# Decode value matmuls in groups of eight and twelve calls, in one fixed order, with nine page buffers

## The chip, the cores and the metric

The kernel runs on one core of a Trainium2 chip. The metric is the device time of that core in microseconds (us); smaller is better. Engines are named as in the profile: PE is TensorE (PEld its weight loads), ACT is ScalarE, DVE is VectorE, POOL is GpSimd, SP is SyncE. POOL and SP also issue DMA transfers, each through its own queue, in the order of their instructions.

## The reference

One step of a hybrid decoder layer, all in float32: a prompt of 512 rows (with 16 learned rows ahead of it) and eight decode sequences of four new rows each. Both go through one input projection, stick-breaking attention with 8 heads of 128, a gated short convolution, and output projections. A decode sequence also reads four pages of 128 old keys and values through a page table.

```python
h = rmsnorm(x, g_pre)
q, k, v, ga, cb, cc, ch, gc, ma, mc = split(h @ w_in)
a = stick_breaking(q, k_past+k, v_past+v) * silu(ga)     # A[t,s] = sigmoid(z_ts) * prod_{s<j<t}(1 - sigmoid(z_tj))
c = cb * causal_conv3(cc * ch) * silu(gc)
merged = sigmoid(ma + b) * (a @ w_pa) + sigmoid(mc + b) * (c @ w_pc)
y = x + rmsnorm(merged @ w_out, g_post)
```

The part that the change touches is the last product of the decode attention, `attn @ v` over the pages: for each of 8 sequences, 2 halves of the 1024 value columns and 4 pages, a product of the weights (128 keys x 32 rows of head and time) with the page (128 keys x 512 columns), plus the product with the sequence's own four new rows.

## The kernel before, in words

Nearly all matmuls are float32 products made of three single-pass products each (high and low parts of both operands). They stand at L256 (`gemm_into`: key, value and query projections, and later `w_pc` and `w_pa`) and at L941 (`product`, used by `seven`, which makes a 2x2 block product with seven instead of eight products). The program runs: start and norm; projections and the first four heads; the gate and convolution stage (L941), with the decode logits on DVE between; then the **w_pc stage**, a loop over `j` of 16 column blocks, each 48 matmuls at L256 into the PSUM tiles `mm` (three buffers), emptied by DVE at L1148. Into this loop the four last prompt heads are put (`head_here`, at `j` = 0, 3, 6, 9: L608 logits, L677 sums, L687 values), and the **decode value matmuls**, L841, through the generator `decode_steps` (`dec_step`). Then come the w_pa stage (L256 on `a_hl`) and the output projection.

A decode value call is of full precision (plain float32): the stationary operand is `A_all` (128 x 32, named `z_all` in the profile), the moving one a page tile `vpage` (128 x 512). The profile shows each call as two matmul records and two weight loads. A call writes 32 of the 128 PSUM partitions of the tile `tp` and takes one of four column groups of the array, `tile_position=(0, 32 * j)`. Over one `po` (a pair of sequence group `g` and column half `hf`) 16 calls with pages and 4 with `v_new` (the new rows) add up; then ACT copies `po` to `ob` (L846), PE transposes it (L849) and DVE multiplies it into `sg_s` (L854). There are four such `po`, so 80 calls. Pages are loaded by POOL (L730, 256 KB each, 64 loads) into `vpage`, which has seven buffers: a load waits until the call that read its buffer has ended.

The order on each engine is made when the program is built, by a scheduler with a model of time: an instruction goes as soon as the model has its inputs ready, the earlier in the code first. `pin` (`keep_in_program_order`) ties an instruction behind what its engine was given just before it in the code. On the chip each engine takes its instructions strictly in that order and waits where an input is late. Before the change the calls are not pinned, so that each is placed where the model has its page landed.

Of the kernel before, what the change touches and what calls it, by code (L numbers as in the profile page):

```python
# [9 lines left out]
F32 = mybir.dt.float32  # L10
# [7 lines left out]
P = 128  # L18
# [26 lines left out]
NPG = 4  # L45
# [15 lines left out]
def hybrid_step_kernel(  # L61
# [7 lines left out]
    pe, act, dve, pool = nc.tensor, nc.scalar, nc.vector, nc.gpsimd  # L69
# [662 lines left out]
    def decode_steps():  # L732
# [89 lines left out]
        for g in range(2):  # L822
            for hf in range(2):
                cs = slice(hf * 512, (hf + 1) * 512)
                po = t_ps()
                for pg in range(NPG + 1):
                    if pg < NPG:
                        vts = []
                        for j in range(4):
                            vt = d3.tile([P, 512], F32, name="vpage", bufs=7)  # L830
                            page_load(vt, vc, 4 * g + j, pg, cs)
                            vts.append(vt)
                        if g + hf + pg == 0:
                            yield "values"
                    for j in range(4):
                        bb = 4 * g + j
                        if pg < NPG:
                            lhs, rhs = A_all[:, pg, bb].rearrange("p h t -> p (h t)"), vts[j]
                        else:
                            lhs, rhs = An[:, bb, :], vflat[:, cs]  # L840
                        pe.matmul(po[32 * j:32 * (j + 1), :], lhsT=lhs, rhs=rhs, start=(pg == 0),  # L841
                                  stop=(pg == NPG), tile_position=(0, 32 * j), skip_group_check=True)
                    if pg < NPG:
                        yield
                ob = d3.tile([P, 512], F32, name="ob")
                act.copy(ob, po)  # L846
                pt = t_ps()
                for hh in range(4):
                    pe.transpose(out=pt[:, hh * P:(hh + 1) * P], in_=ob[:, hh * P:(hh + 1) * P], identity=ident)  # L849
                for hh in range(4):  # L850
                    h = 4 * hf + hh
                    src = pt[:, hh * P:(hh + 1) * P].rearrange("p (j h t) -> p j h t", h=H, t=DT)[:, :, h, :]
                    ss = slice(16 * g, 16 * (g + 1))
                    dve.tensor_mul(sg_s[:, h, ss].rearrange("p (j t) -> p j t", t=DT), src,  # L854
                                   sg_s[:, h, ss].rearrange("p (j t) -> p j t", t=DT))
                yield
# [4 lines left out]
    def dec_step(n=1, until="end"):  # L861

        for _ in range(n):
            if dec_at & {"end", until}:
                return
            dec_at.add(next(dec, "end"))
# [126 lines left out]
        s = sp2.tile([P, 8, P], F32, name="s")  # L993
        yield from seven(ws, n, rb, rt, s, lambda name: sp2.tile([P, HU], F32, name=name)[:, :n])

    gctx = ExitStack()
    gp = gctx.enter_context(tc.tile_pool(name="gates", bufs=2))
    sp2 = gctx.enter_context(tc.tile_pool(name="sums", bufs=1))


    UP, US = PQ + 2, DB * (DT + 2)
# [4 lines left out]
    def conv_pair(i):  # L1006

        def cv(name):
            return [gp.tile([P, 2, HU], F32, tag=name, name=name, bufs=3) for _ in range(2)]

        cc = cv("cv")
        for m, half, b in pair(COL_CC + i * P, HU):
            act.copy(cc[m][:, half, :], b)
        dec_group()
        us_ = [gp.tile([P, UP + US], F32, name="u", bufs=2) for _ in range(2)]
        for m, half, b in pair(COL_CH + i * P, HU):
            u = us_[m]
            up = u[:, 0:UP]
            us = u[:, UP:].rearrange("p (b t) -> p b t", t=DT + 2)
            if half == 0:  # L1020
                dve.tensor_mul(up[:, 2:HU], b[:, 2:HU], cc[m][:, 0, 2:HU])
            else:
                n = PQ - HQ
                dve.tensor_mul(up[:, 0:2], b[:, 0:2], cc[m][:, 1, 0:2])
                dve.tensor_mul(up[:, HU:UP], b[:, 2:2 + n], cc[m][:, 1, 2:2 + n])
                dve.tensor_mul(us[:, :, 2:], b[:, 2 + n:].rearrange("p (b t) -> p b t", t=DT),
                               cc[m][:, 1, 2 + n:].rearrange("p (b t) -> p b t", t=DT))
        dec_group()
        ys = []
        for m in range(2):  # L1030
            u, ii = us_[m], i + m
            up = u[:, 0:UP]
            us = u[:, UP:].rearrange("p (b t) -> p b t", t=DT + 2)
            act.copy(us[:, :, 0:2], stc[:, ii, :].rearrange("p (b r) -> p b r", r=2))
            y = gp.tile([P, 2, HU], F32, tag="cv", name="cv", bufs=3).rearrange("p a b -> p (a b)")[:, 0:TQ]
            for yv, uv, sl in ((y[:, 0:PQ], up, lambda q: (slice(None), slice(q, q + PQ))),
                               (y[:, PQ:TQ].rearrange("p (b t) -> p b t", t=DT), us,
                                lambda q: (slice(None), slice(None), slice(q, q + DT)))):
                dve.tensor_scalar(out=yv, in0=uv[sl(0)], scalar1=wcv[:, 0, ii:ii + 1],
                                  scalar2=wcv[:, 3, ii:ii + 1], op0=ALU.mult, op1=ALU.add)  # L1040
                for q in (1, 2):
                    dve.scalar_tensor_tensor(out=yv, in0=uv[sl(q)], scalar=wcv[:, q, ii:ii + 1], in1=yv,
                                             op0=ALU.mult, op1=ALU.add)
            lt = gp.tile([P, 18], F32, name="lt", bufs=1)
            act.copy(lt[:, 0:2], up[:, PQ:PQ + 2])
            act.copy(lt[:, 2:18].rearrange("p (b r) -> p b r", r=2), us[:, :, DT:DT + 2])
            pt = t_ps()
            pe.transpose(out=pt[0:18, 0:P], in_=lt, identity=ident)
            ln = gp.tile([18, P], F32, name="ln", bufs=1)
            act.copy(ln, pt[0:18, 0:P])  # L1050
            pool.dma_start(conv_prompt[0, 0, :, ii * P:(ii + 1) * P], ln[0:2, :])
            pool.dma_start(conv_sample.rearrange("o b r c -> (o b r) c")[:, ii * P:(ii + 1) * P], ln[2:18, :])
            ys.append(y)
        for m, half, b in pair(COL_GC + i * P, HQ):
            s = by_query(m, half)
            act.activation(b, b, AF.Silu)
            dve.tensor_mul(ys[m][:, s], b, ys[m][:, s])
        dec_group()
        for m, half, b in pair(COL_CB + i * P, HQ):
            s = by_query(m, half)  # L1060
            dve.tensor_mul(ys[m][:, s], b, ys[m][:, s])
        for m in range(2):
            pool.dma_start(c_scr[i + m], ys[m])
        dec_group()
# [12 lines left out]
        dec_group()  # L1077
    for i in range(0, 8, 2):
        conv_pair(i)


    for j in range(0, KD, 2):
# [51 lines left out]
    for j in range(KD):  # L1134
        if j in HERE:
            head_here(HERE[j])
        dec_step(1 + j % 2)
        if j in HERE:
            k = j // 3
            x = sg_load(k)  # L1140
# [291 lines left out]
```

## Time and profile before

| | before |
|---|---|
| median of 3 runs | 1614.03 us (1613.54 to 1615.36) |
| profiled execution, its span | 1615.1 us, 1.1 us above the median |
| PE busy in it | 1595.0 us (99%) |
| granted TensorE clock, mean | 0.997 |
| decode value matmuls, records | 128 with pages, 32 with `v_new`, from 1149.4 to 1301.8 us |
| page loads | 64 of 256 KB, median 5.4 us from issue to landing |

The profiled execution is the source of all durations below; the span is its own time from the first to the last instruction. A busy PE in these views includes the time in which a matmul waits inside the array for the one before it, so two places with a full PE can differ in what they get done.

### The profile page before, as it was taken

The page shows a single profiled execution, that of the slowest core. Times are in us where ns is not written, and L with a number is a line of the kernel's source. Part 1 is how long each engine was busy: PE and PEld are TensorE (multiplying, and loading weights), DVE is VectorE, ACT ScalarE, POOL GpSimd, SP SyncE. Part 2 cuts the span into 40 slices and gives each one's busy share as a digit, 9 for nine tenths or more (in the row PEclk, how much of TensorE's full clock was granted, in tenths as well). Part 3 has the DMA queues.
Part 4 walks back from the last instruction along what each step waited for, and adds up shares of the span by engine and source line. Part 5 has one row for each costly group of instructions (what it writes and reads, how often), then busy time and mean ns, then how long its engine had stood idle before and what let it go on. Part 6 is the DMA issues. An engine that isn't in the chain of part 4 may idle for free.

```text
span 1615.1 us, 32344 instructions
## 1 busy us (share of the span) xinstructions
PE 1595.0 (99%) x12172; PEld 1533.7 (95%) x12172; DVE 1268.6 (79%) x3574; ACT 754.0 (47%) x1339; POOL 238.0 (15%) x428
## 2 busy tenths in 40 slices
PE   9999999999999999999999999999999999999997
PEld 8999999999999999999999999999757789999997
DVE  6328999947899999999999986667565747887776
ACT  6335554435444444444454444446554523355562
POOL 1133333221111001001011100001322210000000
PEclk9999999999999999999999999999999999999999
DMA  8245555344554445454455544444966755533345
GB/s 244 85 139 179 162 173 177 114 121 142 163 166 138 137 139 164 119 151 133 139 171 183 155 145 128 130 127 124 334 218 222 232 152 162 173 88 110 99 133 187
DMA packets 300675, 252.77 MB, mean 157 GB/s; under 512 B 11522, under 2 KB 268614, under 8 KB 299702
## 3 DMA queue, kind: packets, MB, share of 16 engines
q1 hardware_dynamic: 272021, 160.45, 34.5%
q0 software_dynamic: 28368, 89.98, 16.8%
q8 instruction: 95, 1.56, 0.4%
q14 instruction: 63, 0.51, 0.1%
q10 hardware_dynamic: 128, 0.27, 0.1%
HBM read 217.95 MB, written 32.71 MB: 155 GB/s over the span
## 4 chain that ended last, share of the span: by engine, by line
PE 95%; DMA 2%; DVE 2%; ACT 1%; issue 0%; DVEq 0%; POOL 0%; SPq 0%; ACTq 0%
PE mm L941 31%; PE mm L256 27%; PE o L941 23%; PE tp L841 3%; PE mm L321 2%; PE z L677 1%; PE o L687 1%; PE z L321 1%; PE z L608 1%; PE z L1373 1%; DMA sg<-a_scr 1%; PE tp L505 0%; DMA raw<-in_w_pc 0%; DMA qb<-q_scr 0%; PE z L1227 0%
## 5 line engine op out<-in xcount | busy, mean ns | idle before, releaser
L240 ACT CAST whi<-raw 128x1024 fp32r<-128x1024 f32 x247 | 259.5, 1051 | 385.2 <-PE mm L941 118.5
L241 DVE TENSOR_TENSOR wlo<-raw,whi 128x1024 fp32r<-128x1024 f32 x247 | 301.8, 1223 | 87.8 <-ACT whi L240 86.5
L941 PE MATMUL mm<-h_hi,whi 128*128 128x272 f32 (+1 forms) x1152 | 332.3, 288 | 0.0
L941 PE MATMUL mm<-h_lo,whi 128*128 128x272 f32 (+1 forms) x1152 | 332.3, 288 | 0.0
L941 PE MATMUL mm<-h_hi,wlo 128*128 128x272 f32 (+1 forms) x1152 | 332.3, 290 | 0.0
L941 PE MATMUL o<-t_hi,whi 128*128 128x272 f32 (+1 forms) x864 | 250.1, 289 | 1.6 <-DVE c L967 1.6
L941 PE MATMUL o<-t_lo,whi 128*128 128x272 f32 (+1 forms) x864 | 250.2, 290 | 0.0
L754 DVE CUSTOM_DVE_ANT_0 junk<-kpage,qb 128x128 f32<-128x128 f32 x1024 | 246.3, 288 | 4.7 <-DMA qb<-q_scr 4.3
L941 PE MATMUL o<-t_hi,wlo 128*128 128x272 f32 (+1 forms) x864 | 249.8, 289 | 0.0
L941 PEld LDWEIGHTS mm<-h_hi,whi 128*128 128x128 f32 x1152 | 217.4, 189 | 0.0
L941 PEld LDWEIGHTS mm<-h_hi,wlo 128*128 128x128 f32 x1152 | 216.8, 189 | 0.1
L941 PEld LDWEIGHTS mm<-h_lo,whi 128*128 128x128 f32 x1152 | 216.8, 188 | 0.1
L241 DVE TENSOR_TENSOR wlo<-s,whi 128x1024 fp32r<-128x1024 f32 x126 | 154.4, 1225 | 63.6 <-ACT whi L240 62.4
L240 ACT CAST whi<-s 128x1024 fp32r<-128x1024 f32 x126 | 132.0, 1048 | 153.8 <-PE mm L941 51.7
L256 PE MATMUL mm<-h_lo,whi 128*128 128x280 f32 (+1 forms) x640 | 187.6, 293 | 0.0
L256 PE MATMUL mm<-h_hi,wlo 128*128 128x280 f32 (+1 forms) x640 | 187.1, 293 | 0.0
L256 PE MATMUL mm<-h_hi,whi 128*128 128x280 f32 (+1 forms) x640 | 186.7, 292 | 0.0
L941 PEld LDWEIGHTS o<-t_hi,whi 128*128 128x128 f32 x864 | 163.0, 189 | 2.1 <-DVE c L967 2.0
L941 PEld LDWEIGHTS o<-t_lo,whi 128*128 128x128 f32 x864 | 163.4, 189 | 0.4 <-issue 0.4
L941 PEld LDWEIGHTS o<-t_hi,wlo 128*128 128x128 f32 x864 | 163.1, 189 | 0.1
L256 PEld LDWEIGHTS mm<-h_lo,whi 128*128 128x128 f32 x640 | 120.3, 188 | 0.8
L256 PEld LDWEIGHTS mm<-h_hi,whi 128*128 128x128 f32 x640 | 120.5, 188 | 0.5
(390 smaller groups left out, 3214.5 us busy)
## 6 DMA issues: line engine op xcount, KB each, us to landing
raw<-in_w_in SPq DMA_DIRECT2D x192, 512.0 KB, 4.3
kpage<-in_cache_k POOLq DMA_DIRECT2D x64, 256.0 KB, 3.7
qb<-q_scr POOLq DMA_DIRECT2D x32, 512.0 KB, 5.7
vpage<-in_cache_v POOLq DMA_DIRECT2D x64, 256.0 KB, 5.4
raw<-in_w_out SPq DMA_DIRECT2D x32, 512.0 KB, 4.1
gate_scr<-g POOLq DMA_DIRECT2D x32, 272.0 KB, 4.8
gt<-gate_scr POOLq DMA_DIRECT2D x16, 544.0 KB, 4.5
raw<-in_w_pc SPq DMA_DIRECT2D x16, 512.0 KB, 7.3
```

Source lines behind the costliest of these rows:

```text
L240: act.copy(hi, x)
L241: dve.tensor_sub(lo, x, hi.bitcast(F32))
L256: pe.matmul(o, lhsT=w, rhs=r[:, t0:t1], start=(k == 0 and n == 0), stop=(k == nk - 1 and n == 2))
L321: pin(pe.matmul(o, lhsT=l, rhs=r[:, k, t0:t1], start=(start and m == 0), stop=(stop and m == 2), skip_group_check=True))
L608: pe.matmul(zt[:m, c0:c0 + n], lhsT=l[:, s0:s0 + m], rhs=r[:, ts:ts + n], start=(c0 == 0 and i == 0), stop=(i == 2), skip_group_check=True)
L677: pe.matmul(o, lhsT=l, rhs=x, start=False, stop=(i == len(ops) - 1), skip_group_check=True)
L687: pe.matmul(ot[:, ts - NMETA:ts - NMETA + n], lhsT=l[:m, st, :], rhs=x[:m, c0:c0 + n], start=False, stop=(g == GROUPS[-1] and i == 2), ski ...
L754: dve.tensor_tensor_reduce(out=junk, in0=kt[:, h * P:(h + 1) * P], in1=qt[:, t, h * P:(h + 1) * P], scale=1.0, scalar=0.0, op0=ALU.mult, o ...
L841: pe.matmul(po[32 * j:32 * (j + 1), :], lhsT=lhs, rhs=rhs, start=(pg == 0), stop=(pg == NPG), tile_position=(0, 32 * j), skip_group_check= ...
L941: pe.matmul(o, lhsT=l[:, k, :], rhs=r, start=(start and k == 0 and m == 0), stop=(stop and k == 7 and m == 2), skip_group_check=True)
L1373: pin(pe.matmul(o, lhsT=(m1, m2)[h][:, k + 8 * (q == 1), ts], rhs=two[h][q == 2][:, :, k, :], start=(n == 0), stop=(n == 47)))
```

## The change

The calls over two pages are now handed over together: eight in the first half of a `po`, and twelve in the second (eight with pages and the four with `v_new`). All are pinned, so the scheduler can put nothing between them. In a group the calls stand in the reverse of the order of loading, so that the page loaded last comes first; the column group runs 3, 2, 1, 0, 3, 2, 1, 0. `vpage` has nine buffers instead of seven. The generator now yields 8 times after "values" instead of 20, and the loop over `j` takes one step per `j` instead of one or two. To make room for the buffers, the pools of the gate and convolution stage are put in another order, and the tiles `u`, `lt` and `ln` go to a pool of their own (`convu`), which is closed after the convolution.

```diff
-                for pg in range(NPG + 1):
-                    if pg < NPG:
-                        vts = []
+                def pages(vts, last):
+                    for n, (lhs, rhs, pg, j) in enumerate(vts):
+                        pin(pe.matmul(po[32 * j:32 * (j + 1), :], lhsT=lhs, rhs=rhs, start=(pg == 0),
+                                      stop=last and n >= len(vts) - 4, tile_position=(0, 32 * j), skip_group_check=True))
+
+                for pp in range(0, NPG, 2):
+                    vts = []
+                    for pg in (pp, pp + 1):
                         for j in range(4):
-                            vt = d3.tile([P, 512], F32, name="vpage", bufs=7)
+                            vt = d3.tile([P, 512], F32, name="vpage", bufs=9)
                             page_load(vt, vc, 4 * g + j, pg, cs)
-                            vts.append(vt)
...
-                        pe.matmul(po[32 * j:32 * (j + 1), :], lhsT=lhs, rhs=rhs, start=(pg == 0),
-                                  stop=(pg == NPG), tile_position=(0, 32 * j), skip_group_check=True)
-                    if pg < NPG:
+                            vts.insert(0, (A_all[:, pg, 4 * g + j].rearrange("p h t -> p (h t)"), vt, pp, j))
+                    if g + hf + pp == 0:
+                        yield "values"
+                    if pp == 0:
+                        vts[4:] = [(l, r, 1, j) for l, r, _, j in vts[4:]]
+                    else:
+                        vts += [(An[:, 4 * g + j, :], vflat[:, cs], NPG, j) for j in reversed(range(4))]
+                    pages(vts, pp > 0)
+                    if pp == 0:
                         yield
...
-    gctx = ExitStack()
+    gctx, uctx = ExitStack(), ExitStack()
+    sp2 = gctx.enter_context(tc.tile_pool(name="sums", bufs=1))
     gp = gctx.enter_context(tc.tile_pool(name="gates", bufs=2))
-    sp2 = gctx.enter_context(tc.tile_pool(name="sums", bufs=1))
+    up_ = uctx.enter_context(tc.tile_pool(name="convu", bufs=2))
...
-        dec_step(1 + j % 2)
+        dec_step(1)
```

The built order on PE before the change, in the second of the four `po`, at the end of the first prompt head of the loop (`mm` is the w_pc product, `z` and `o` a prompt head, `tp` the decode value product):

```order
L687 MATMUL o<-loA,vhi 128x512
L687 MATMUL o<-hiA,vlo 128x512
L841 MATMUL tp<-vpage,z_all 32x512
L256 MATMUL mm<-c_hl,whi 128x272
L256 MATMUL mm<-c_hl,wlo 128x272
L256 MATMUL mm<-c_hl,whi 128x272 x2
L841 MATMUL tp<-vpage,z_all 32x512
L256 MATMUL mm<-c_hl,wlo 128x272
L256 MATMUL mm<-c_hl,whi 128x272 x2
```

And on PE after the change, at the end of the first `po` (its second group), where the sums of the second head stand ahead of it:

```order
L677 MATMUL z<-lo,neg_u 128x400
L256 MATMUL mm<-c_hl,whi 128x272 x2
L256 MATMUL mm<-c_hl,wlo 128x272
L256 MATMUL mm<-c_hl,whi 128x272 x2
L256 MATMUL mm<-c_hl,wlo 128x272
L256 MATMUL mm<-c_hl,whi 128x272
L829 MATMUL tp<-vpage,z_all 32x512 x8
L829 MATMUL tp<-v_new,z_new 32x512 x4
L256 MATMUL mm<-c_hl,whi 128x272
L256 MATMUL mm<-c_hl,wlo 128x272
```

Before, single calls stand between w_pc matmuls; now all 80 calls stand in eight such unbroken pieces. The first piece, which stood ahead of the first head's work after 72 w_pc matmuls, now comes after that head's last L687. In the matmuls of other lines that stand between one piece and the next, the new order has 99, 77, 69, 82, 89, 74 and 82.

On POOL before the change (`gate_scr<-gt` stores a finished w_pc product and waits for DVE), each load follows the one call that frees its buffer:

```order
L730 DMA vpage<-in_cache_v 128x512
L1149 DMA gate_scr<-gt 128x544
L730 ISA
L730 DMA vpage<-in_cache_v 128x512
L730 ISA
```

On POOL after the change, ahead of the third group's loads (shown with numbers, since the page tiles of one group have neighbouring ones: 15625 is the last of the second group, 15712 the first of the third):

```order
L730 DMA vpage_15625<-in_cache_v 128x512
L730 ISA
L730 DMA vpage_15712<-in_cache_v 128x512
L1154 DMA gate_scr_890<-gt_16454 128x544
L1154 DMA gate_scr_890<-gt_16554 128x544
L730 ISA
L730 DMA vpage_15714<-in_cache_v 128x512
```

Eight of the nine buffers belong to a group, so only the first page of the next group can be asked for before the group's calls have run; its other seven are asked for behind the calls. Of such stores the new order has 0, 2, 1, 1, 2, 0 and 2 between a group's calls and the last load of the next group.

On PE at the end of the stage, after the change, the last head's values and the first w_pa matmuls (`a_hl`):

```order
L687 MATMUL o<-hiA,vlo 128x512
L256 MATMUL mm<-c_hl,wlo 128x272
L256 MATMUL mm<-c_hl,whi 128x272 x2
...
L852 MATMUL tp<-ident,ob 128x128 x4
L256 MATMUL mm<-c_hl,whi 128x272 x2
L256 MATMUL mm<-c_hl,wlo 128x272
L256 MATMUL mm<-a_hl,whi 128x272 x2
```

Ten w_pc matmuls and the four transposes stand between the two now; before it was 97 w_pc matmuls.

More of the change, by code (lines that the diff above doesn't have):

```diff
@@ L825, in decode_steps @@
                 po = t_ps()
-                for pg in range(NPG + 1):
-                    if pg < NPG:
-                        vts = []
+                def pages(vts, last):
[5 more added lines that the diff above has]
+                    for pg in (pp, pp + 1):
                         for j in range(4):
-                            vt = d3.tile([P, 512], F32, name="vpage", bufs=7)
+                            vt = d3.tile([P, 512], F32, name="vpage", bufs=9)
                             page_load(vt, vc, 4 * g + j, pg, cs)
-                            vts.append(vt)
[L833 to L836, printed above, removed]
-                        if pg < NPG:
[L838 to L841, printed above, removed]
-                                  stop=(pg == NPG), tile_position=(0, 32 * j), skip_group_check=True)
-                    if pg < NPG:
+                            vts.insert(0, (A_all[:, pg, 4 * g + j].rearrange("p h t -> p (h t)"), vt, pp, j))
[7 more added lines that the diff above has]
+                    if pp == 0:
                         yield
@@ L1014, in conv_pair @@
         dec_group()
-        us_ = [gp.tile([P, UP + US], F32, name="u", bufs=2) for _ in range(2)]
+        us_ = [up_.tile([P, UP + US], F32, name="u", bufs=2) for _ in range(2)]
         for m, half, b in pair(COL_CH + i * P, HU):
@@ L1043, in conv_pair @@
                                              op0=ALU.mult, op1=ALU.add)
-            lt = gp.tile([P, 18], F32, name="lt", bufs=1)
+            lt = up_.tile([P, 18], F32, name="lt", bufs=1)
             act.copy(lt[:, 0:2], up[:, PQ:PQ + 2])
@@ L1048, in conv_pair @@
             pe.transpose(out=pt[0:18, 0:P], in_=lt, identity=ident)
-            ln = gp.tile([18, P], F32, name="ln", bufs=1)
+            ln = up_.tile([18, P], F32, name="ln", bufs=1)
             act.copy(ln, pt[0:18, 0:P])
@@ L1079, in hybrid_step_kernel @@
         conv_pair(i)
+    uctx.close()
     for j in range(0, KD, 2):
```

## Prediction

> **What bounds the kernel now.** I read the page's parts 1 and 4 first, then the records of line L841 (the decode value calls) in two stretches, then the timeline of PE at those calls. The page has the span, the busy time of each engine, and the chain of work that ended last by engine and by line:
>
> ```profile
> span 1615.1 us, 32344 instructions
> PE 1595.0 (99%) x12172; PEld 1533.7 (95%) x12172; DVE 1268.6 (79%) x3574; ACT 754.0 (47%) x1339; POOL 238.0 (15%) x428
> PE 95%; DMA 2%; DVE 2%; ACT 1%; issue 0%; DVEq 0%; POOL 0%; SPq 0%; ACTq 0%
> PE mm L941 31%; PE mm L256 27%; PE o L941 23%; PE tp L841 3%; PE mm L321 2%; PE z L677 1%; PE o L687 1%; PE z L321 1%; PE z L608 1%; PE z L1373 1%; DMA sg<-a_scr 1%; PE tp L505 0%; DMA raw<-in_w_pc 0%; DMA qb<-q_scr 0%; PE z L1227 0%
> ```
>
> PE is the bound, and the value calls are themselves on the chain (3% of the span). So time taken off PE there comes off the end, as long as nothing else is late. L841's busy time alone, by stretch (busy time, records, loads, clock, DMA share, GB/s):
>
> ```profile
> 1149.00:1158.00 9.00, 1.91 (x12) 0.39 (x12) 0.81 1.05 356
> 1158.00:1303.00 145.00, 45.55 (x148) 6.40 (x148) 1.00 0.71 222
> ```
>
> Six calls (12 records) cost 1.91 us in the first stretch; the other 74 take 45.55 us. That they differ so much per call (0.32 and 0.62 us) is the matter of this change. The timeline of PE shows why: a lone call, then four calls in a row, then four with pages and four with the new rows (start, duration from the first start to the last end, count of records):
>
> ```profile
> 1163.52 0.28 PE L256 MATMUL mm<-c_hl,wlo 128*128 128x272 f32 x1
> 1163.73 1.05 PE L841 MATMUL tp<-vpage,z_all 128*32 128x512 f32 x2
> 1164.71 0.52 PE L256 MATMUL mm<-c_hl,whi 128*128 128x272 f32 x2
> 1165.06 0.29 PE L256 MATMUL mm<-c_hl,wlo 128*128 128x272 f32 x1
> ...
> 1247.52 0.29 PE L256 MATMUL mm<-c_hl,wlo 128*128 128x272 f32 x1
> 1247.73 1.06 PE L841 MATMUL tp<-vpage,z_all 128*32 128x512 f32 x8
> 1248.73 0.52 PE L256 MATMUL mm<-c_hl,whi 128*128 128x272 f32 x2
> 1249.09 0.28 PE L256 MATMUL mm<-c_hl,wlo 128*128 128x272 f32 x1
> ...
> 1255.31 1.06 PE L841 MATMUL tp<-vpage,z_all 128*32 128x512 f32 x8
> 1256.30 1.06 PE L841 MATMUL tp<-v_new,z_new 32*32 32x512 f32 x8
> 1257.30 0.52 PE L256 MATMUL mm<-c_hl,whi 128*128 128x272 f32 x2
> ```
>
> One call holds the array from 1163.73 to 1164.71; four calls in the four column groups hold it from 1247.73 to 1248.73. Four cost what one costs, and a second round of four adds 0.99 us (1255.31 to 1256.30).
>
> **The change part by part.** First the unit: in steady work 320 matmuls take 40.00 us, 0.125 us each.
>
> ```profile
> 1360.00:1400.00 40.00, 40.00 (x320) 40.00 (x320) 29.85 (x64) 15.58 (x26) 3.71 (x7) 1.00 0.62 189
> ```
>
> Around the lone call, L256 at 1163.52 to L256 at 1165.06 is 1.54 us with three w_pc steps in it (0.375), so a lone call costs 1.165 us: its 1.05 busy and 0.115 of switching in and out. The same at the four calls: 1.57 - 0.375 = 1.195. A group of eight is then 1.195 + 0.99 = 2.185, one of twelve 3.175.
>
> *Removed and put in its place.* After 1158 the 74 calls stand in 39 separate pieces: 45.55 + 39 x 0.115 = 50.0 us. Afterwards 80 calls stand in eight pieces: 4 x 2.185 + 4 x 3.175 = 21.4 us. The difference is **-28.6 us**. The first six calls of before give nothing, since they ran inside a stall that stays:
>
> ```profile
> 1149.36 1.91 PE L841 MATMUL tp<-vpage,z_all 128*32 128x512 f32 x12
> 1154.53 0.82 PE L256 MATMUL mm<-c_hl,whi 128*128 128x272 f32 x2 [3.25 <-DVE gt L1148]
> 1155.14 0.43 PE L256 MATMUL mm<-c_hl,wlo 128*128 128x272 f32 x1
> 1157.41 0.51 PE L256 MATMUL mm<-c_hl,whi 128*128 128x272 f32 x2
> 1142.59 10.63 DMA sg<-a_scr
> ```
>
> The last row is of the chain in order of time: PE waits for DVE to empty `mm`, and DVE waits for a 256 KB load that took 10.63 us. After the change PE has 72 w_pc matmuls, then nothing, until the same moment.
>
> *The first wait.* Nine page loads instead of seven now go out while that load is on its way, in a stretch in which the DMA engines are full:
>
> ```profile
> 1130.00:1140.00 10.00, 10.00 (x76) 9.79 (x75) 6.03 (x9) 6.45 (x10) 2.70 (x5) 1.00 1.09 338
> 1140.00:1150.00 10.00, 10.00 (x84) 9.48 (x84) 5.85 (x9) 9.97 (x18) 4.55 (x7) 1.00 1.08 351
> ```
>
> Two pages are 0.52 MB, at 351 GB/s up to 1.5 us more; but the loads that came at 1150.7 before, behind the first calls, are then gone. Bounds -1 to +1.5; I take **+0.5**, since the full share is the nearest row. After such an idle time the clock is low: from 1154.53 to 1157.41 there are 13 matmuls, 2.88 us instead of 1.63. That 1.25 us is paid before and after alike.
>
> *Waits for pages.* This is the new wait: the whole piece waits for eight pages, and everything behind it on PE with it (w_pc, the heads, then w_pa). POOL's timeline has the nearest case, seven loads freed at once, and the landing times of all pages:
>
> ```profile
> 1234.80 3.78 POOL L730 DMA_DIRECT2D vpage<-in_cache_v  x6 [10.35 <-PE tp L841]
> 1238.97 0.54 POOL L730 DMA_DIRECT2D vpage<-in_cache_v  x1 [0.39 <-issue]
> 1239.52 0.55 POOL L1149 DMA_DIRECT2D gate_scr<-gt  x1
> DMA to landing us min/median/max: 2.8/5.4/7.6
> ```
>
> The seventh load goes out 4.2 us behind the first and lands 5.4 to 7.6 us later. With 1.0 us until the group's first four calls have freed their buffers, the next group is complete 10.6 to 12.8 us from its predecessor's start, plus 0.55 per store that stands ahead in POOL's queue (none, 2, 1, 1, 2, none, 2). What PE has to do until it gets there: 99, 77, 69, 82, 89, 74 and 82 matmuls at 0.125, plus the piece itself: 14.6, 12.8, 10.8, 13.4, 13.3, 12.4 and 12.4 us. So the waits are 0, 0 to 1.1, 0.4 to 2.6, 0, 0 to 0.6, 0 to 0.4 and 0 to 1.5: 0.4 to 6.2 in all. I take **+2.5**, nearer to the median landing. Nine buffers, the reverse order and the smaller step count cost nothing else: the first piece comes behind 310 w_pc matmuls, 39 us of work, and its pages were asked for ahead of these, and a wait at the first call of a piece covers those of the other seven.
>
> [...]
>
> *Chains of the heads.* Lone calls were cover for ACT and DVE too: between the second head's last L608 and the first L677 that needs the chain's result, PE took 20 us, and ACT gave that result at 1207.83; now 83 w_pc matmuls, 10.4 us, stand there.
>
> ```profile
> 1197.71 0.17 PE L608 MATMUL z<-qhi,klo 128*16 128x16 f32 x1
> 1217.70 0.34 PE L677 MATMUL z<-hi,neg_u 128*128 128x400 f32 x1
> 1207.83 0.53 ACT L494 CAST hi<-r 128x416 fp32r<-128x416 f32 x1
> 1313.82 0.69 DVE L1119 TENSOR_TENSOR sg<-o,sg 128x512 f32<-128x512 f32 x1 [3.75 <-PE o L687]
> 1315.90 0.69 DVE L495 TENSOR_TENSOR a_hl<-sg,a_hl 128x512 fp32r<-128x512 f32 x1
> ```
>
> 1208.36 - 1197.88 is 10.5 us: just in time, without the 9 us that were spare. At the stage's end the last head's output needs 2.8 us (1313.82 to 1316.59); ten w_pc matmuls, four transposes and 21 of w_pa cover it with about 4.4. Bounds 0 to 2 us for each of four heads; I take **+2** in all.
>
> *Pools.* The early part of the stage at L941 is put in a slightly other order (`u`, `sums`). PE is full there, so 0, within 1 us.
>
> The sum on the profiled execution: 1615.1 - 28.6 + 0.5 + 2.5 + 2 = 1591.5. It lies 1.1 above the median of the runs, so the forecast is **1590 us**, 1.5% less.
>
> **The rivals.** *Pages bind (B).* If the page loads get only half of the DMA engines throughout, seven of them (1.83 MB at half of 338 GB/s) need 10.9 us, from 1.0 us behind the start and with the 2.8 of the shortest landing: 14.7. The waits are then 0.1, 1.9, 3.9, 1.3, 1.4, 2.3 and 2.3, 13 us instead of 2.5 (the stores go out meanwhile): **1601 us**. For it: the stage's bytes stay, while its time shrinks. Against it: the share after 1158 is only 0.71. [...]
>
> *Cold array (C), the slower side.* If each of the seven waits passes 3.25 us, the idle time at which the trace shows the clock fall, each costs 3.3 + 1.25 us, 32 in all, and with the terms of the first wait and of the heads that is more than the gain: 1614.0 - 28.6 + 32 + 2.5, **1620 us**. It decides from 3.7 us per group, (28.6 - 2.5) / 7, clock included; the share just named speaks against it.
>
> *No packing (D).* Each call in a group waits for its own page; if that kept the calls apart, 80 calls of 0.98 us would cost 79 us, against 50 now: **1644 us**. The four calls at 1247.73 had four pages too, and overlapped.
>
> *Cover gone (E).* The heads and the emptying of `mm` eat the gain: 7 us at each of four heads, **1614 us**. DVE is busy for 93 of the 152 us of this stretch, and could stand 124:
>
> ```profile
> 1149.40:1301.80 152.40, 149.15 (x888) 102.25 (x887) 93.02 (x209) 71.78 (x125) 37.81 (x70) 0.99 0.73 230
> ```
>
> *Better (F).* The load of the first wait comes 1 us earlier, and no piece or chain waits: **1584 us**.
>
> **How the numbers follow.** Forecast 0.62 (own range 1585 to 1596), B 0.20, C 0.05, D 0.03, E 0.05, F 0.05. The range, 1584 to 1604, holds the forecast, F's edge and most of B. About 0.2% (3 us) is what a measurement of this kernel tells from no change. Faster by more: forecast, B and F, 0.87; within: E, with a little of B's tail, 0.05; slower: C and D, 0.08.
>
> **What would show it.** L829 should be eight pieces with about 20.5 us busy, each piece's first record alone with an idle time in front. POOL's waits for PE at `vpage` should fall from 27 to about seven. A piece that runs over 2.2 (eight) or 3.2 us (twelve), idle PE of over 1 us ahead of most pieces, a clock under 1.0 after 1160, or L677 and L687 waiting for ACT or DVE would make the terms wrong in that order.

## The result, and the profile after

The changed kernel takes 1597.6 us (median of 4 runs, 1596.9 to 1598.9), the kernel before on the same chip 1614.7 (1613.5 to 1618.5). The ratio is 0.9897, 95% interval 0.9882 to 0.9913: 17 us faster, where 24 were forecast. Of all the executions behind this document three took 2572, 3063 and 4180 us, and the ratios leave them out. The profiled execution has a span of 1597.3 us against 1615.1.

The page after has the span and the busy time; then comes line L829 (the value calls, L841 of before) in the two stretches used for before (busy time and records of PE, the same of weight loads, granted clock, DMA share, GB/s):

```profile
span 1597.3 us, 32319 instructions
PE 1567.6 (98%) x12172; PEld 1533.7 (96%) x12172; DVE 1268.8 (79%) x3574; ACT 752.7 (47%) x1339; POOL 234.6 (15%) x428
```

```profile
1149.00:1158.00 9.00, 0.00 (x0) 0.00 (x0) 0.76 0.87 290
1158.00:1303.00 145.00, 18.86 (x160) 4.03 (x160) 0.97 0.77 244
```

The same 160 records stand there, in 18.9 us instead of 47.5 (19.4 with the end of the last group, which this stretch cuts off), and no call is left in the first wait. PE's timeline shows one group of eight and one of twelve:

```profile
1200.39 0.40 PE L687 MATMUL o<-hiA,vlo 128*128 128x512 f32 x1
1200.71 1.92 PE L829 MATMUL tp<-vpage,z_all 128*32 128x512 f32 x16
1202.57 0.18 PE L608 MATMUL z<-qhi,klo 128*16 128x16 f32 x1
...
1219.07 0.29 PE L256 MATMUL mm<-c_hl,whi 128*128 128x272 f32 x1
1219.29 1.92 PE L829 MATMUL tp<-vpage,z_all 128*32 128x512 f32 x16
1221.14 1.06 PE L829 MATMUL tp<-v_new,z_new 32*32 32x512 f32 x8
1222.13 0.39 PE L256 MATMUL mm<-c_hl,whi 128*128 128x272 f32 x1
1222.37 0.29 PE L256 MATMUL mm<-c_hl,wlo 128*128 128x272 f32 x1
```

From the w_pc matmul at 1219.07 to the one at 1222.37 is 3.30 us with two w_pc steps in it (0.25), so a group of twelve holds PE for 3.05; eight calls take 0.99 less, 2.06. Four of each are 20.4 us, where 21.4 were forecast and 50.0 stood before. PE's busy time in the whole span fell by 27.4 us (1595.0 to 1567.6), the span by 17.8. What is missing is idle time, and matmuls that ran slowly, which count as busy. The stage of the change shows both, in PE's timeline (in square brackets the idle time ahead, and what ended it) and in windows (stretch, length, busy time of PE, PEld, DVE, ACT and POOL, granted clock, DMA share, GB/s):

```profile
1154.34 0.82 PE L256 MATMUL mm<-c_hl,whi 128*128 128x272 f32 x2 [5.79 <-DVE gt L1153]
...
1179.96 0.52 PE L256 MATMUL mm<-c_hl,whi 128*128 128x272 f32 x2 [2.05 <-DVE gt L1153]
...
1211.42 0.63 PE L256 MATMUL mm<-c_hl,whi 128*128 128x272 f32 x2 [2.29 <-DVE gt L1153]
```

```profile
1140.00:1150.00 10.00, 8.56 (x69) 8.34 (x67) 4.97 (x8) 9.52 (x16) 4.91 (x8) 1.00 1.05 368
1150.00:1160.00 10.00, 5.66 (x25) 5.66 (x26) 5.61 (x10) 0.66 (x2) 0.56 (x1) 0.68 0.86 271
1180.00:1185.00 5.00, 5.00 (x28) 5.00 (x29) 3.55 (x11) 1.49 (x3) 0.54 (x1) 0.66 0.62 191
1206.00:1211.00 5.00, 3.13 (x25) 2.91 (x24) 0.97 (x3) 3.44 (x6) 1.47 (x3) 1.00 0.99 314
1211.00:1216.00 5.00, 4.58 (x24) 4.58 (x25) 3.95 (x9) 2.32 (x4) 0.54 (x1) 0.66 0.96 353
```

All three waits are for the same thing: DVE's multiply of `gt`, which empties `mm`. Behind each of them the granted clock is low (0.68, 0.66 and 0.66 in the windows that begin at 1150, 1180 and 1211). The chain of waits says what kept DVE at the first, DVE's timeline what kept it at the third, and the waits summed over 1139 to 1308 (us in total, times, longest) say how little PE waited for pages:

```profile
1141.71 11.32 DMA sg<-a_scr
1153.15 0.70 DVE sg L1124
1153.85 0.45 DVE gt L1153
1154.34 5.81 PE mm L256 x24
```

```profile
1210.92 0.79 DVE L1153 TENSOR_TENSOR gt<-mm,gt 128x272 f32<-128x272 f32 x2 [4.03 <-DMA gt<-gate_scr]
```

```profile
POOL vpage L730 <- PE tp L829: 39.6, 8, 9.3
PE mm L256 <- DVE gt L1153: 10.1, 3, 5.8
PE tp L829 <- DMA vpage<-in_cache_v: 1.4, 2, 0.7
```

At 1154 the multiply of `gt` stood on DVE behind one that waited 11.3 us for `a_scr`. At 1180 it stood behind a head's chain (DVE was busy without a gap from 1174 on), and at 1211 it waited for a gate tile that SP had asked for only at 1204.01, in the midst of eight page loads (POOL issued them from 1202.06 to 1206.93).

### The profile page after: what moved, and what is told of

It reads as the page before. It is cut to its first block, busy times and chain, and to the rows that moved or that the text cites. A ratio compares the mean times of both kernels' runs of the same rounds, so it can differ in the third digit from the quotient of the medians.

```text
span 1597.3 us, 32319 instructions
## 1 busy us (share of the span) xinstructions
PE 1567.6 (98%) x12172; PEld 1533.7 (96%) x12172; DVE 1268.8 (79%) x3574; ACT 752.7 (47%) x1339; POOL 234.6 (15%) x428
## 4 chain that ended last, share of the span: by engine, by line
PE 89%; DMA 4%; issue 2%; DVE 2%; ACT 1%; POOL 0%; DVEq 0%; POOLq 0%; SPq 0%; ACTq 0%
PE mm L944 32%; PE mm L256 24%; PE o L944 23%; DMA vpage<-in_cache_v 2%; PE mm L321 2%; PE z L321 1%; PE z L677 1%; PE o L687 1%; DMA raw<-in_w_in 1%; PE z L608 1%; PE z L1378 1%; DMA sg<-a_scr 1%; DMA gt<-gate_scr 1%; DVE wlo L241 1%; PE tp L829 0%
```

## The experiments

For each run the ratio is to the kernel before, on the same chip. Beside it I give the length of the stage in the profiled execution, from the start of the first w_pc matmul to that of the last w_pa matmul: 282.1 us before, 265.2 after. It leaves out what differs from execution to execution earlier on (the first w_pc matmul came between 1135.8 and 1140.6 in these traces). Every edit makes the planner, as the scheduler of the build is called below, place the groups anew: the first group stands behind 310 w_pc matmuls after the change, behind 328 with buffers of their own, and behind 269 with the first pages held back. So two runs differ in more than the edit alone.

**The pools and buffers alone.** The kernel before, with `bufs=9` for `vpage` and the three pools changed:

```
-                            vt = d3.tile([P, 512], F32, name="vpage", bufs=7)
+                            vt = d3.tile([P, 512], F32, name="vpage", bufs=9)
-        us_ = [gp.tile(...)]; lt = gp.tile(...); ln = gp.tile(...)
+        us_ = [up_.tile(...)]; lt = up_.tile(...); ln = up_.tile(...)
```

> The kernel before with the changed kernel's nine page buffers and its new pools, but the value calls page by page and not pinned, as before. Theory (the time follows the number of pieces): this order has the 80 calls in 34 pieces, where the order of before has 40; with 0.98 us for a round of up to four calls and 0.2 for switching that is some 7 us less, so about 1607 us. Rival 1 (buffers and pools carry the gain, through pages that come earlier): 1600 or less. Rival 2 (buffers and pools do nothing): 1614.7 within 2.

Measured: 0.9988 (0.9975 to 1.0001), 1613.2 us, stage 281.9. The calls became 6.3 us shorter, as the planner set more of them together, yet the stage stayed as long. The groups of L841 in the stage (busy time, mean ns of one), and a row of PE's timeline:

```profile
L841 PE MATMUL tp<-vpage,z_all 128*32 128x512 f32 x128 | 37.2, 611 | 0.0
L841 PE MATMUL tp<-v_new,z_new 32*32 32x512 f32 x32 | 4.2, 600 | 0.0
```

```profile
1257.42 0.49 PE L677 MATMUL z<-lo,neg_u 128*128 128x400 f32 x1 [2.18 <-DVE lo L495]
```

Before, the two lines have 42.4 and 5.3 us. The first wait grew to 4.6 us from 3.25 and a new one of 2.2 came, each with low clock behind it (0.50 in the windows from 1152 to 1158 and from 1258.42 to 1260.42). So the theory held for the calls and failed for the time: calls standing alone had covered waits, and what packing saves is first paid back to those. The prediction's term for the pools, 0 within 1, lies inside this interval (-4.0 to +0.2 us); but the run has the shorter calls in it too, so it does not show the pools by themselves.

**The order in the group turned round.**

```
-                            vts.insert(0, (A_all[:, pg, 4 * g + j]..., vt, pp, j))
+                            vts.append((A_all[:, pg, 4 * g + j]..., vt, pp, j))
-                        vts += [(An[:, 4 * g + j, :], ..., NPG, j) for j in reversed(range(4))]
+                        vts += [(An[:, 4 * g + j, :], ..., NPG, j) for j in range(4)]
```

> The changed kernel with only the order inside a group turned round: the page loaded first comes first. Theory (grouping alone does it; my prediction put the reverse order at no cost and no gain): 1597.6 within 1.5. Rival (the reverse order is what keeps a group in one piece, since its first call waits for the last page and the other calls then have nothing to wait for, while in forward order the planner puts w_pc and head work between the calls): its order has 31 pieces instead of 8, 48.8 us by rounds of 0.99 and 0.2 per piece instead of 21.4; with some 5 us of the new idle times covered again, about 1620, no faster than before.

Measured: 1.0012 (1.0001 to 1.0024), 1615.9 us, stage 281.8: the whole gain is gone. The built order on PE, a little behind the first group's first nine calls, and the groups of L829 in the profile:

```order
L829 MATMUL tp<-vpage,z_all 32x512
L256 MATMUL mm<-c_hl,wlo 128x272
L256 MATMUL mm<-c_hl,whi 128x272 x2
L256 MATMUL mm<-c_hl,wlo 128x272
L256 MATMUL mm<-c_hl,whi 128x272 x2
L256 MATMUL mm<-c_hl,wlo 128x272
L256 MATMUL mm<-c_hl,whi 128x272 x2
L256 MATMUL mm<-c_hl,wlo 128x272
L256 MATMUL mm<-c_hl,whi 128x272
L829 MATMUL tp<-vpage,z_all 32x512
```

```profile
L829 PE MATMUL tp<-vpage,z_all 128*32 128x512 f32 x128 | 39.3, 601 | 0.0
L829 PE MATMUL tp<-v_new,z_new 32*32 32x512 f32 x32 | 4.2, 600 | 0.0
```

43.5 us of calls instead of 19.6. `pin` keeps calls in their order but, other than the section on the change says, does not keep other work out from between them. With the page loaded first in front, each call waits for its own page and the planner fills the gaps with w_pc. With the page loaded last in front, nothing is left to wait for behind the first call, and the group stays whole. So the reverse order, to which the prediction gave no price, carries the change.

**Groups of four.** One page of each of four samples to a group (the last of a pass eight, with the new rows):

```
-                for pp in range(0, NPG, 2):
+                for pg in range(NPG):
...
-        dec_step(1)
+        dec_step(1 + j % 2)
```

> The changed kernel with one page of each of four samples to a group (four calls, the last group of a pass with the new rows eight) in place of two pages; its order has 12 pieces, 4 or 8 calls each. Theory (number of pieces counts, bursts of loads little): 12 pieces cost 0.8 us more than 8; about 1598.5, within 2. Rival (eight page loads at a time delay the loads of the heads and gates behind them): bursts halve, the idle times of 2.0 and 2.3 us at 1180 and 1211 and their low clock (3.1 us) go, 1590 to 1593.

Measured: 0.9935 (0.9913 to 0.9956), median 1605.3; its runs lie in two clusters, 1599.6 to 1601.0 and 1605.3 to 1606.3. The profiled execution is of the lower, with a stage of 268.8, 3.6 longer than after. There the last group came after w_pc had ended, with nothing left to cover it:

```profile
1303.77 1.94 PE L829 MATMUL tp<-vpage,z_all 128*32 128x512 f32 x8 [3.56 <-DMA vpage<-in_cache_v]
1305.63 1.93 PE L829 MATMUL tp<-v_new,z_new 32*32 32x512 f32 x8
```

The rival's time, 1590 to 1593 us, did not come. Its mechanism stays open, though: this trace has no stall near 1211, and an idle time of 2.30 us at 1177 cost no clock (1.00 in the windows from 1175 to 1187), while the late end came with 3.56 us of idle time and a clock of 0.50 in the windows from 1304 to 1314. The 0.8 us for more pieces is not to be told apart from that end, and what separates the two clusters stays open, since no trace of the upper one was taken.

**Page loads left out.** All groups use the first group's eight pages:

```
+                            if g + hf + pp == 0:
                                 vt = d3.tile([P, 512], F32, name="vpage", bufs=9)
                                 page_load(vt, vc, 4 * g + j, pg, cs)
+                                kept.append(vt)
+                            vt = kept[4 * (pg - pp) + j]
```

> The changed kernel with the eight pages of the first group used by all groups: 56 of the 64 page loads are left out (all value calls stay, on wrong pages). Its order has 5 pieces, 0.6 us less than 8. Theory (page loads cost the two page waits, 1.4 us, and by their bursts the late gate load at 1211 with its low clock, some 4 us; the other idle times come from the heads' chains on DVE and stay): about 1592. Rival 1 (page loads are hidden but for 1.4 us): 1595.5. Rival 2 (all new idle time, 9.5 us and 5 of low clock, comes from page traffic): 1583 to 1585.

Measured: 0.9829 (0.9809 to 0.9848), 1588.0 us, stage 255.4, 9.7 less than after: between the theory and its second rival. Windows with the columns of before (busy time of PE, PEld, DVE, ACT and POOL, clock, DMA share, GB/s):

```profile
1165.00:1190.00 25.00, 23.88 (x190) 23.30 (x188) 18.79 (x39) 13.93 (x23) 1.63 (x3) 1.00 0.63 189
1190.00:1215.00 25.00, 25.00 (x195) 19.03 (x194) 16.17 (x39) 16.01 (x29) 1.08 (x2) 1.00 0.58 174
```

There is no idle time from 1190 to 1215, and the clock is 1.00 in both windows. The first wait is still there (5.8 us), since the first eight pages are still loaded ahead of it. So the 56 later loads cost up to 9 us in all, though PE waits for pages themselves for only 1.4; that the rest comes by way of other loads that they hold up, and of the clock, is my estimate. The order of the groups differs here too (five pieces), which these numbers do not separate.

**The first piece ahead of the first head.**

```
+    dec_step(1)
     for j in range(KD):
...
-        dec_step(1)
+        if j:
+            dec_step(1)
```

> The changed kernel with the first group's calls ahead of the first head of the stage in program order instead of behind it: its eight calls then stand right before the first wait (behind 69 w_pc matmuls), all other groups move up by one place. In the changed kernel's trace the eight pages have landed at 1148.2, and the wait is from 1148.55 to 1154.34. Theory (what a piece costs is paid only where PE has other work): its 2.05 us vanish in the wait, the loads of the second group start 50 us earlier and no longer meet the gate load that was late at 1211 (2.3 us idle, 1.5 of low clock): 1597.6 - 2.05 - 3.8 = 1592. Rival 1 (only the piece itself is hidden): 1595.5. Rival 2 (the eight page loads that follow at 1150 delay the head's loads and the gate loads of the first head): 1598 or more.

Measured: 0.9889 (0.9872 to 0.9905), 1598.1 us, stage 269.1. The expectation was built on a misreading. I had counted rows of the order as matmuls; behind 69 rows stand 102 w_pc matmuls, so the piece fell behind the wait, not into it. The wait was 6.64 us, a new one of 3.90 came at 1253, and one of 2.04 at 1211 was for a head's sums, so the run tests neither the theory nor its rivals. The same misplacing holds for the run that joins this with the next edit:

> The changed kernel with both: the first group's calls ahead of the first head, and two buffers of their own for sg_scr and a_scr. Theory: the first wait, cut to some 2 us, is filled by the piece (2.05): 1588 - 2 = 1586, the best of these. Rival (the second group's eight loads at 1150 collide with gate and head loads, which now matter): 1588 to 1592.

Measured: 0.9841 (0.9824 to 0.9857), 1589.0 us, stage 255.0: no different from the next edit alone.

**Buffers of their own for `sg_scr` and `a_scr`.**

```
+    sgp = cctx.enter_context(tc.tile_pool(name="sgs", bufs=2))
...
-        sg = g3.tile([P, 2, TQ], F32, tag="gt", name="sg")
+        sg = sgp.tile([P, 2, PQ], F32, name="sg")
```

> The changed kernel with the tiles that take sg_scr and a_scr in two buffers of their own, so that the four buffers of the pool at L1110 are for the gate tiles alone; in its order the first three multiplies of gt, which empty mm, come on DVE ahead of the multiply that waits for a_scr. Theory (the first wait is the a_scr load, 11.3 us, ahead of gt on DVE; the gate load late at 1211 was late for want of a buffer): the first wait shrinks from 5.8 us to at most 2, its low clock (3 us) goes or halves, and the stall at 1211 (2.3 + 1.5) goes: 1597.6 - 3.8 - 2 - 3.8 = 1588. Rival 1 (the gate loads come as late as a_scr, since the DMA engines are full to 1154): the first wait stays, 1593 to 1594. Rival 2 (both stalls are moved behind another buffer): 1597 or more.

Measured: 0.9848 (0.9826 to 0.9870), 1591.2 us, stage 256.6. The stalls at 1180 and 1211 are gone, with PE busy to the full there, but the first wait stays at 4.2 us, now for the gate tile (windows with PE's busy time, the clock, DMA share and GB/s; a row of the chain of waits; one of DVE's timeline):

```profile
1175.00:1190.00 15.00, 15.00 (x116) 1.00 0.60 189
1190.00:1215.00 25.00, 25.00 (x196) 1.00 0.71 237
```

```profile
1140.37 12.12 DMA gt<-gate_scr
```

```profile
1152.61 1.14 DVE L1154 TENSOR_TENSOR gt<-mm,gt 128x272 f32<-128x272 f32 x3 [7.32 <-DMA gt<-gate_scr]
```

Theory and first rival each hold for one place. At 1211 the gate load was late for want of a buffer: SP asked for the stage's seventh gate tile at 1204.01 after the change, and at 1172.52 here. At 1150 the gate load comes as late as the load of `a_scr` did, in a stretch with a DMA share of 1.05, behind the nine page loads. The next run asks whether these are the reason.

**The first nine page loads held back.** Each of the first eight page tiles first takes one element of the first gate tile, so that its load, and the ninth load behind it in POOL's queue, waits until that tile has landed. The first steps of the generator move to the same place:

```
                             vt = d3.tile([P, 512], F32, name="vpage", bufs=9)
+                            if g + hf + pp == 0:
+                                pool.tensor_copy(vt[0:1, 0:1], gt_at[0][0:1, 0:1])
...
         nc.sync.dma_start(gt, gate_scr[j][:, 1, :])
+        if j == 0:
+            gt_at.append(gt)
+            dec_step(64, "values")
+            dec_step(1)
```

> The changed kernel with the first nine page loads held back until the first gate tile of the stage has landed (each page tile first takes one element of that gate tile). In the changed kernel these pages are asked for from 1136.3 to 1142.9, while the load of a_scr (1141.7, 11.3 us) is under way, and the first group uses them at 1200. Theory (the first wait is the DMA engines' queue, and the pages are much of it: 2.36 MB, 6.7 us at 351 GB/s): a_scr's load takes 5 to 7 us, the first wait falls from 5.8 us to 0.5 to 1.5, and its low clock (3.3 us) goes: 1597.6 - 4.5 - 3.3 = 1590. Rival (the loads of SP's own queue fill the engines to 1152 anyway): the wait stays above 4 us, 1596 to 1598.

Measured: 0.9841 (0.9825 to 0.9858), 1590.0 us as expected, stage 256.6. The load of `a_scr` that took 11.3 us was there within 3.9 (issued at 1140.07), and the first wait is gone. SP's and DVE's rows, then the windows of PE:

```profile
1140.07 0.42 SPq L1149 DMA_DIRECT2D sg<-a_scr  x1
1143.91 0.69 DVE L1126 TENSOR_TENSOR sg<-sg 128x512 f32<-128x512 f32 x1 [0.58 <-DMA sg<-a_scr]
```

```profile
1140.00:1150.00 10.00, 10.00 (x82) 1.00 0.98 313
1150.00:1160.00 10.00, 10.00 (x80) 1.00 0.96 342
```

That is against 8.56 and 5.66 us of busy time after the change, at clock 1.00 and 0.68. The pages were in nobody's need: the first group uses them at 1200 after the change, and at 1188 here. The DMA engines are as full as the first rival said (share 0.98 and 0.96), yet the load came early, so it was the page loads that had held it up.

That the time came out as expected is in part luck. In place of the first wait PE now idles for 1.79 and 2.58 us up to 1169 and 1172, both times for a head's sums (the longer in the row below, of the waits), with 6.83 us at half clock (0.50 in the windows from 1170.28 to 1176.24), and for 1.37 us at 1206. Against that the stall at 1180 is gone, and the one at 1211 is down to this 1.37.

```profile
PE z L677 <- DVE lo L495: 2.6, 1, 2.6
```

**Both.**

> The same, and sg_scr and a_scr in two buffers of their own. There the first wait was 4.2 us behind the gate load (1140.4, 12.1 us), with 2 us lost to the low clock after it. Theory: with the pages held back the gate load takes 5 to 7 us, the wait and its low clock go, and no idle time of over 2 us is left: 6 us less than with the buffers alone, a ratio to the kernel before of 0.981 (1584 on a 1614.7 of before). Rival (as above): ratio 0.985, no better than the buffers alone.

Measured: 0.9806 (0.9780 to 0.9832), 1587.4 us, stage 253.7. PE has no idle time from 1140 to 1160 and the longest in the stage is 1.9 us, at clock 1.00. This is the fastest of the kernels run, some 15 us ahead of the changed kernel by the ratios.

**The clock behind the first wait.** First 14 matmuls that compute nothing needed, and the first group behind them:

```
+            if j == 1 and o is oc[1]:
+                warm = cp.tile([P, P], F32R, name="warm")
+                act.copy(warm, oc[0][:, 0:P])
+                for _ in range(14):
+                    pe.matmul(po_at[0], lhsT=warm, rhs=neg_one...broadcast_to([P, 4, P]), start=True, stop=True, ...)
```

> The changed kernel with 14 matmuls that compute nothing needed (128x512, some 0.22 us each, 3.1 in all) behind the first 72 w_pc matmuls, in the first wait, and with the first group's calls behind those, in the same wait: PE then idles for under 1 us there instead of 5.79. Theory (the low clock after the wait comes from the idle time, not from what follows): clock 1.00 from 1154 on, some 3 us saved by that beside the 2.05 of the piece: about 1592.5, or 1588.7 if the loads of the second group no longer meet the gate load at 1211. Rival (the low clock comes from a limit on work or on current that the stage's start sets off): clock 0.5 for some 6 us all the same, 1595.5 to 1597.6.

> The kernel with the 14 idle-time matmuls and the first piece in the first wait once more, for its profile, since the first profile of it was of a disturbed execution. Theory (low clock comes from idle time): idle under 1.5 us and clock 1.00 behind the first wait. Rival: clock 0.5 for some 6 us all the same.

Measured: 0.9869 (0.9852 to 0.9885), 1594.7 us. The profile is of another execution (1591.7 us, stage 260.2). It shows that the test missed its place: the matmuls stand behind the 107th w_pc matmul, 8.5 us after the wait's end, where they cost time:

```profile
1152.15 0.82 PE L256 MATMUL mm<-c_hl,whi 128*128 128x272 f32 x2 [5.84 <-DVE gt L1166]
...
1160.63 3.35 PE L1160 MATMUL tp<-neg_one,warm 128*128 128x512 f32 x14
```

It decides nothing on the clock. It is faster than the changed kernel all the same: its groups come at other places, and its trace has no stall at 1180 and one of 1.25 us near 1211. That this is the reason is a reading, not shown by a run. Then 22 such matmuls, pinned between the last w_pc matmul ahead of the wait and the first behind it:

```
+                for _ in range(22):
+                    pin(pe.matmul(po_at[0], lhsT=neg_one, rhs=neg_one...broadcast_to([P, 4, P]), ...))
...
+                    if j == 1 and (o is oc[1] and k == n == 0 or o is oc[0] and k == 7 and n == 2):
+                        pin(x)
```

> The changed kernel with 22 matmuls that compute nothing needed (128x512, 0.24 us each by the 14 that took 3.35, so 5.3 in all) right behind the 72nd w_pc matmul, this time inside the first wait, where PE otherwise does nothing for 5.79 us; the groups come one step of the loop later in program order. PE then idles for 0.5 us there, and the w_pc matmuls start again at the same moment as before, when DVE has emptied mm. Theory (the low clock behind the wait comes from the idle time): clock 1.00 from the start of w_pc's 73rd matmul on; the 3.3 us that the low clock costs there go and nothing else changes at that place: 1594.3, ratio to the kernel before 0.9877, and the stage from the first w_pc matmul to the last of w_pa 261.9 us long instead of 265.2, less or more what the moved groups do. Rival 1 (the low clock is set off by something else, such as the change from idle to dense work or the loads): clock 0.5 for some 6 us there, 1597.6, ratio 0.9897. Rival 2 (the clock of later idle times of about 2 us falls more often after a warm start): 1596 to 1598 with clock 1.00 at the first wait.

Measured: 0.9839 (0.9822 to 0.9855), 1589.3 us, stage 258.5. PE's timeline, and the windows behind it:

```profile
1145.64 5.18 PE L1158 MATMUL tp<-neg_one 128*128 128x512 f32 x22
1152.72 0.52 PE L1163 MATMUL mm<-c_hl,whi 128*128 128x272 f32 x2 [1.90 <-DVE gt L1170]
1153.08 0.28 PE L1163 MATMUL mm<-c_hl,wlo 128*128 128x272 f32 x1
1153.20 0.29 PE L1163 MATMUL mm<-c_hl,whi 128*128 128x272 f32 x1
```

```profile
1150.00:1155.00 5.00, 2.63 (x15) 1.91 (x13) 3.47 (x8) 0.62 (x1) 0.56 (x1) 1.00 0.59 171
1155.00:1160.00 5.00, 4.89 (x40) 3.92 (x44) 3.23 (x7) 1.40 (x3) 0.00 (x0) 1.00 0.92 264
```

The clock is 1.00 from the first matmul behind the wait on, where two matmuls start 0.12 us apart (1153.08 and 1153.20), while the changed kernel has 24 in 5.81 us there, 0.24 each. So the low clock there comes from the idle time (5.79 us there, 1.90 here), and rival 1 falls. The changed kernel's own trace agrees: its clock fell at 1153.64, before the first matmul behind the wait at 1154.34, so it was not the return to dense work that set it off. Rival 2 was not met: no later window is low, but no later idle time is over 1.20 us either. The time is better than the theory gave; here too the stalls at 1180 and 1211 are absent with the groups moved. So the clock is priced by the rows of the traces, not by this ratio.

## Why the prediction was right, and what it mis-sized

The way and the main term came as forecast: calls set together cost less, and PE was hardly held up by pages. The time itself lies above the 1585 to 1596 us that the forecast gave itself, in the part of its range that was kept for rival B, whose waits did not come. To that extent the range held by luck; the terms say where the missing 7 us went.

*Removed and put in its place* (-28.6): right, -29.6 by the rows above. Eight pieces, none broken.

*The reverse order "cost nothing else"*: true, and it missed the point. The groups of eight that the term counts on exist only by it; without it the time is that of before.

*Waits for pages* (+2.5): 1.4, in two waits. Rival B, pages that bind, did not come. No run shows the half share of the DMA engines on which its sum is built; the median landing of a page went from 5.4 us before to 5.8 after. The shortest landing before, the 2.8 us in that sum, came at a DMA share of 0.47 (1193.69 to 1196.49).

*Pools* (0): 0.9988 with its interval reaching 1.0001 does not contradict it; no run has the pools alone with the calls unchanged.

*The first wait* (+0.5, the low clock "paid before and after alike"): the idle part is right (5.79 against 3.25 and the 1.91 of calls that had run inside it, +0.6). The clock is not alike. Before, 13 matmuls took 2.88 us; now 24 take 5.81 (the chain's row), 2.8 lost instead of 1.25: +1.5. The clock was at half for 6.83 us instead of 3.41. The calls that had stood in the wait had kept the array from idling for so long.

*Chains of the heads* (+2): here the prediction failed in size, and in the place. The heads' own sums stalled PE once, by 1.2 us. What stalled it was the emptying of `mm`: DVE's multiply of `gt` came 2.05 us late at 1180, behind the head's work on DVE, and 2.29 us late at 1211, behind a gate load. Each time the clock fell to 0.50 for 3.41 us, some 1.5 lost. That is 5.5 of idle and 3.0 of clock, 8.5 in place of 2. The prediction had priced the heads' chains by what their own sums need, and none of its signs looked at the emptying of `mm` by a DVE that is busy with a head or waits for a load; its share of busy time, 93 of 152 us, does not show that.

The sum so corrected is -29.6 + 0.6 + 1.5 + 1.4 + 8.5 = -17.6; the stage became 16.9 shorter, and nothing outside it moved by more than a microsecond. Rival C had the right mechanism at the wrong waits: it let the clock fall only behind 3.25 us. Rival E, cover that is gone, was real at under a third of the price it was given (8.5 of 28). That the late `gt` comes from shared buffers at 1211, and from the page loads at the first wait, is shown by the rows of the runs with buffers of their own and with the pages held back. Their ratios, 0.984 to 0.985 for each alone and 0.981 for both, agree, but have the moved groups in them. At 1180 the two causes, DVE's order and the page traffic, were not told apart.

## What to carry to other kernels

Before counting a gain from packing work on the bounding engine, look for what the scattered work had covered: list every wait on the results that it empties (here the three `mm` banks), and price each uncovered wait twice, once as idle time and once as the slow clock behind it (at the first wait here 5.79 us idle, and 2.8 lost behind it). To keep a group of calls whole under a scheduler, put the call whose input comes last in front; tying the calls to one order is not enough. And loads that are needed 50 us later should not be sent while one that is needed now is under way (here that one took 11.3 us, and 3.9 with the nine page loads held back).

## What the runs showed of the hardware

An idle time of PE need not reach 3.25 us to be followed by a low clock. In the stage of the changed kernel the granted clock was 0.50 from 1153.64 to 1160.46, from 1180.94 to 1184.36 and from 1211.66 to 1215.08, that is for 6.83, 3.41 and 3.41 us, and 1.00 in between. The idle times at these places were 5.79, 2.05 and 2.29 us. The one of 2.05 us ended at 1179.96, and the clock fell when PE had been back at work for 1 us:

```profile
1179.96:1180.96 1.00, 1.00 (x8) 0.99 1.15 347
1180.96:1181.96 1.00, 1.00 (x7) 0.50 0.93 188
```

Of six idle times between 2.0 and 2.3 us, four were followed by a clock of 0.50 (2.05 and 2.29 after the change, 2.18 with the pools alone, 2.04 with the first piece ahead). Two were not (2.02 with the order turned round, 2.30 with groups of four): there the clock was 1.00 in the windows of the 7 us behind. Why these two, the traces don't show. PE's timeline and a window of the run with groups of four, where 2.30 us kept the clock:

```profile
1177.22 0.52 PE L256 MATMUL mm<-c_hl,whi 128*128 128x272 f32 x2 [2.30 <-DVE gt L1150]
```

```profile
1177.00:1182.00 5.00, 4.78 (x38) 1.00 0.63 199
```

With groups of four, a round of four calls in the four column groups took 1.86 us to the start of the next round at a clock of 0.50 (1303.77 to 1305.63 above), and 0.99 before the change at 1.00. And the median landing of the 272 KB gate loads issued from 1138 to 1152 (four in each trace) was 11.0 us behind the nine page loads (buffers of their own alone) and 3.3 with these held back (both edits). The rows of DMA issues, in that order of the two kernels:

```profile
gt<-gate_scr SPq DMA_DIRECT2D x4, 272.0 KB, 11.0
```

```profile
gt<-gate_scr SPq DMA_DIRECT2D x4, 272.0 KB, 3.3
```
